# A hybrid decoder step on one core: RMS norms found on the whole row instead of on columns of tokens

## The chip, the core and the metric

The kernel runs on 1 core of a Trainium2 chip. The metric is device time in microseconds (us) for one execution; runs of the kernel before and of a changed kernel are taken on the same chip. The kernel before has a median of 1988.76 us over 3 runs (1988.32 to 1993.46).

## What is computed

One layer of a hybrid decoder for 2048 prompt tokens and 8 sample tokens (2056 in all, 1024 features, float32): RMSNorm; an input projection of 1024 by 1024, whose first half drives a state space mixer (32 groups, 64 complex states) and whose second half a causal pooling mixer; an output projection with residual; RMSNorm; a gated feed-forward part with a causal convolution of width 3 (up to 2 x 2816 columns, down to 1024) with residual; a last RMSNorm. The function at issue is the norm, which stands at three places:

```python
def _rmsnorm(x, g):
    xf = x.astype(jnp.float32)
    y = xf * lax.rsqrt(jnp.mean(xf * xf, axis=-1, keepdims=True) + EPS)
    return (y * g.astype(jnp.float32)).astype(x.dtype)
```

## The kernel before

All activations lie transposed: features on the 128 partitions (8 tiles of them), tokens along the free axis. A token's sum of squares is therefore a sum over 8 tiles and over 128 partitions. Big products are done in three float32r matmuls each (high and low parts, `mm3`, L82 to L89); the parts are made by `split` (L74 to L76: the high part on ScalarE, the low part on VectorE or GpSimd).

The stages, in order of time:

- Start and input projection (to some 300 us). Tokens in 5 pieces (`SUBS`: 512, 512, 512, 264, 256). `prep_x(i)` loads a piece, splits it and finds its norm. For pieces 0 and 1 ScalarE squares each tile and GpSimd adds the squares up per partition (`acc`), and `rstd_from` (L125) turns them into the factor of every token. Pieces 2, 3 and 4 take the sums from rows in natural order (`stats`, L189) and go to `rstd_bcast` (L104) directly. The state space mixer runs in the background of this stage and the next.
- Output projection (some 300 to 605 us). Tokens in 8 pieces (`CSUBS`: 256 each, one of 264). `out_proj(i)` makes x1 tile by tile (L920), squares and sums it (L922 to L926); `norm_out(i)` finds the norm, scales the 8 tiles (L948) and stores them (L950). The last piece's norm is found at once into `rs_last` (L938) and used later.
- Up projection with convolution (some 600 to 1505 us): a Strassen-Winograd scheme with 7 products instead of 8. `prep_h` reloads the normed rows and makes sums and splits of them; `prep_w` does it for the weights.
- Down projection (some 1505 us to the end), 7 products again. `residual` squares and sums the new rows (L1314 to L1321); `final(c)` (L1328) finds the last norm of each of the 8 pieces and scales and stores the output, after the products `p7` (four pieces) and `p4` (four pieces).

`rstd_from` is thus called for 18 norms: 2 of 512 columns, 14 of 256 and 2 of 264. It works on columns of tokens: for each block of 128 tokens, the squares are the weights of a matmul with one column of ones (L133), which puts one token's sum on one partition. `rstd_bcast` then works on 128 x (2 to 4) values: mean and eps (L110), root on ScalarE (L111), reciprocal (L112), one step of Newton (L113 to L116), then per block a diagonal matrix of the factors (L121) and a matmul with ones (L122) that gives every partition all factors, and a copy out of PSUM (L123). The tile of PSUM for both (tag `ms`) exists once, and is shared with the mixer's transposes; the diagonals have two buffers.

The order of each engine's instructions is made by a planner that simulates the program by a cost model and priorities; tiles are reused after their release, and every engine runs its own queue in order. SyncE issues nearly all DMAs, in one queue, in order too.

Of the kernel before, what the change touches and what calls it, by code (L numbers as in the profile page):

```python
# [9 lines left out]
F32 = mybir.dt.float32  # L10
F32R = mybir.dt.float32r
I32 = mybir.dt.int32
AF = mybir.ActivationFunctionType
ALU = mybir.AluOpType
# [4 lines left out]
D = 1024  # L19
# [9 lines left out]
EPS = 1e-6  # L29
# [15 lines left out]
def build(tc, a):  # L45
    nc = tc.nc
    V, S, P, T, Y = nc.vector, nc.scalar, nc.gpsimd, nc.tensor, nc.sync
    es = ExitStack()
    with es:
# [72 lines left out]
                T.matmul(ps[:, b * 128:b * 128 + w], lhsT=ones, rhs=dg[:, :w], start=True, stop=True)  # L122
            S.copy(out=out, in_=ps[:, :n])  # L123

        def rstd_from(accs, out, n):  # L125
            nb = (n + 127) // 128
            ps = psm[0].tile([128, 512], F32, tag="ms", name="ps_st")
            if n % 128:
                V.memset(ps[:, 0:nb], 1.0)
            for b in range(nb):  # L130
                w = min(128, n - b * 128)
                for x, acc in enumerate(accs):
                    T.matmul(ps[0:w, b:b + 1], lhsT=acc[:, b * 128:b * 128 + w], rhs=ones[:, 0:1],  # L133
                             start=x == 0, stop=x == len(accs) - 1)
            rstd_bcast(ps[:, 0:nb], out, n)

        ypair = {}

# [36 lines left out]
        with ExitStack() as er_:  # L175
# [37 lines left out]
            def prep_x(i):  # L213
                t0, n = SUBS[i]
                tiles = []
                nat = i in NAT
                if nat:
                    st = stats(i)
                else:
                    acc = sp.tile([128, 512], F32, tag="dec", name="acc", bufs=2)  # L220
                for k in range(KT):
                    if i < 2:
                        tag = ("H", "tab", "U", "M1", "tm", "yg", "t2", "kt")[k]
                        raw = sp.tile([128, 512], F32, tag=tag, name="xraw", bufs=2 if k < 3 else 1)
                    else:
                        raw = xp.tile([128, 512], F32, tag="xraw", name="xraw", bufs=3)
                    Y.dma_start(out=raw[:, :n], in_=a["xT"][k, :, t0:t0 + n])
                    if i < 4:
                        pool = xp if i % 2 else xpa
                        hi = pool.tile([128, 520], F32R, tag=f"xh{k}", name="xh", bufs=1)  # L230
                        lo = pool.tile([128, 520], F32R, tag=f"xl{k}", name="xl", bufs=1)
                        pair[k] = (hi, lo)
                    else:
                        hi, lo = (t[:, SUBS[3][1]:] for t in pair[k])
                    split_scaled(hi[:, :n], lo[:, :n], raw[:, :n], col(C_G1, k))
                    tiles.append((hi[:, :n], lo[:, :n]))
                    if nat:
                        st(k)
                    elif k == 0:
                        S.activation(out=acc[:, :n], in_=raw[:, :n], func=AF.Square)  # L240
                    else:
                        sq = xp.tile([128, 512], F32, tag="sq", name="sq")
                        S.activation(out=sq[:, :n], in_=raw[:, :n], func=AF.Square)
                        P.tensor_tensor(out=acc[:, :n], in0=acc[:, :n], in1=sq[:, :n], op=ALU.add)
                xr[i] = tiles
                if i == 0:
                    Y.dma_start(out=ident, in_=a["ident"])
                if i < 4:
                    rs = pair["rs"] = xp.tile([128, 520], F32, tag="rstd", name="rstd", bufs=2)
                else:  # L250
                    rs = pair["rs"][:, SUBS[3][1]:]
                if nat:
                    rstd_bcast(st(None), rs[:, :n], n)
                else:
                    rstd_from([acc[:, :n]], rs[:, :n], n)
                rst[i] = rs

            Y.dma_start(out=cst, in_=a["cst"])
# [598 lines left out]
        if True:  # L857
# [14 lines left out]
            def ct(tag, dt=F32, bufs=1, pool=None):  # L872
                return (pool or c2).tile([128, 256 if pool is c3 else CW], dt, tag=tag, name=tag, bufs=bufs)
# [37 lines left out]
            def out_proj(i, g, nxt):  # L911
                t0, n = CSUBS[i]
# [22 lines left out]
                    if i == len(CSUBS) - 1 and d % 2:  # L935
                        Y.dma_start(out=x1_d[i][:, d - 1:d + 1], in_=x1[:, d - 1:d + 1, :n])
                if i == len(CSUBS) - 1:
                    rstd_from([acc[:, :n]], rs_last, n)  # L938
                else:
                    pend.append(lambda: norm_out(i, x1, acc))  # L940

            def norm_out(i, x1, acc):
                t0, n = CSUBS[i]
                Y.dma_start(out=x1_d[i], in_=x1[:, :, :n])
                rs = ct("rs")
                rstd_from([acc[:, :n]], rs[:, :n], n)
                for d in range(KT):
                    V.scalar_tensor_tensor(out=x1[:, d, :n], in0=x1[:, d, :n], scalar=col(C_G2, d), in1=rs[:, :n],  # L948
                                           op0=ALU.mult, op1=ALU.mult)
                Y.dma_start(out=xn_d[i], in_=x1[:, :, :n])  # L950
# [289 lines left out]
        with ExitStack() as ed:  # L1240
# [86 lines left out]
            def final(c, top):  # L1327
# [1 line left out]
                rs = d2.tile([128, 264], F32, tag="rs", name="rs")  # L1329
                low = d2.tile([128, 4, 264], F32, tag="low", name="low")  # L1330
                Y.dma_start(out=low[:, :, :n], in_=x2_d[c])
                rstd_from(ssq[c] if isinstance(ssq[c], list) else [ssq[c][:, :n]], rs[:, :n], n)
                if c == 2 * len(UNITS) - 2:
                    for h, x in enumerate((low, top)):
                        for d in range(4):
# [146 lines left out]
```

## Time and profile before

| | |
|---|---|
| median of 3 runs | 1988.76 us (1988.32 to 1993.46) |
| profiled execution | 1997.34 us, span 1995.5 us |
| TensorE (PE) busy | 1877.3 us, 94% |
| VectorE (DVE) busy | 1404.4 us, 70% |
| ScalarE (ACT) busy | 898.1 us, 45% |
| GpSimd (POOL) busy | 904.7 us, 45% |
| mean granted TensorE clock | 0.973 |

The profile is one execution. The span runs from the first to the last instruction that it records. "Busy" counts an engine's instructions, not waits. An entry in square brackets behind an instruction is the time for which its engine stood idle before it, with what ended that. PEld is TensorE's weight load, SPq a DMA that SyncE issues. Matmuls overlap, so that their spacing, and not their length, says what one costs. A float32 matmul shows as two records.

### The profile page before, as it was taken

The numbers are of one execution on the slowest core, as the hardware profiler recorded it, in microseconds if no ns is written. First come the engines' busy times: TensorE is split into PE (matmuls) and PEld (weight loads), VectorE is DVE, ScalarE is ACT, GpSimd is POOL, SyncE is SP. The second block draws the span as 40 slices with busy tenths as digits, with TensorE's granted clock in tenths as the row PEclk, the third lists the DMA queues.
The fourth block names the chain that finished last, engine by engine and source line by source line (L and its number), as shares of the span: only waits on it lengthen the run. The fifth ranks groups of instructions, "written<-read, shape, count | busy, mean of one in ns | idle before, by whom it ended". The sixth has DMA issues, their size and how long they took to land.

```text
span 1995.5 us, 38363 instructions
## 1 busy us (share of the span) xinstructions
PE 1877.3 (94%) x14680; PEld 1815.0 (91%) x14680; DVE 1404.4 (70%) x2423; ACT 898.1 (45%) x1666; POOL 904.7 (45%) x1091
## 2 busy tenths in 40 slices
PE   6888997999998999999997999999998999999998
PEld 4667876999988999999997999999998989999997
DVE  8888576875588777787789777777775343444675
ACT  5333224544445555555565555555554332322332
POOL 4365662211156455445457555445531165134651
PEclk9989998999999999999998999999998999999999
DMA  6456666865453433233334233323317574356663
GB/s 218 159 165 176 189 179 214 224 176 154 130 178 115 132 122 117 91 112 101 96 102 142 90 114 99 100 87 117 97 60 267 173 248 147 103 189 212 227 205 120
DMA packets 214215, 296.61 MB, mean 149 GB/s; under 512 B 41216, under 2 KB 157824, under 8 KB 213776
## 3 DMA queue, kind: packets, MB, share of 16 engines
q1 hardware_dynamic: 201104, 285.76, 45.3%
q10 hardware_dynamic: 12928, 8.41, 1.5%
q8 instruction: 115, 1.88, 0.4%
q14 instruction: 68, 0.56, 0.1%
HBM read 199.60 MB, written 93.32 MB: 147 GB/s over the span
## 4 chain that ended last, share of the span: by engine, by line
PE 55%; POOL 4%; DVE 4%; DMA 3%; issue 3%; ACT 1%; DVEq 0%; POOLq 0%; ACTq 0%; SPq 0%
PE ps_X L1147 8%; PE ps_X L1146 8%; PE ps_X L1145 8%; PE ps_d L88 4%; PE ps_d L87 4%; PE ps_d L89 4%; PE ps_Z L1146 4%; PE ps_Z L1147 4%; PE ps_Z L1145 4%; PE ps_Y L1147 2%; PE ps_Y L1145 2%; PE ps_Y L1146 2%; DMA x_d<-xo 1%; DMA wr<-w_dn 1%; POOL xo L1307 1%
## 5 line engine op out<-in xcount | busy, mean ns | idle before, releaser
L87 PE MATMUL ps_d<-bh,wh 128*128 128x256 f32 (+1 forms) x1232 | 346.0, 285 | 12.5 <-ACT bh L75 12.5
L88 PE MATMUL ps_d<-bl,wh 128*128 128x256 f32 (+1 forms) x1232 | 349.3, 285 | 6.3 <-DVE bl L76 6.3
L89 PE MATMUL ps_d<-bh,wl 128*128 128x256 f32 (+1 forms) x1232 | 348.5, 284 | 0.0
L76 DVE TENSOR_TENSOR wl<-raw,wh 128x512 fp32r<-128x512 f32 x308 | 270.5, 881 | 64.0 <-ACT wh L75 61.5
L75 ACT CAST wh<-raw 128x512 fp32r<-128x512 f32 x308 | 189.7, 619 | 236.7 <-PE ps_X L1146 166.8
L1173 DVE SCALAR_TENSOR_TENSOR ps_cv<-hup,cst,ps_cv 128x512 f32<-128x512 f32 x352 | 258.1, 750 | 53.1 <-ACT ps_cv L1171 50.9
L1080 POOL TENSOR_TENSOR raw<-raw 128x512 f32<-128x512 f32 x176 | 241.4, 1372 | 83.7 <-DVE wl L76 68.3
L87 PEld LDWEIGHTS ps_d<-bh,wh 128*128 128x128 f32 x1232 | 233.1, 191 | 13.5 <-ACT bh L75 13.5
L88 PEld LDWEIGHTS ps_d<-bl,wh 128*128 128x128 f32 x1232 | 234.7, 191 | 7.4 <-DVE bl L76 7.4
L89 PEld LDWEIGHTS ps_d<-bh,wl 128*128 128x128 f32 x1232 | 235.0, 191 | 0.0
L76 DVE TENSOR_TENSOR bl<-br,bh 128x1536 fp32r<-128x1536 f32 (+3 forms) x56 | 112.4, 2008 | 101.0 <-ACT bh L75 94.0
L1171 ACT ACTIVATE ps_cv<-hup,cst 128x512 f32<-128x512 f32 x176 | 135.9, 782 | 8.3 <-DVE hup L1133 3.9
L87 PE MATMUL ps_in<-xh,wh 128*128 128x512 f32 (+2 forms) x288 | 110.0, 383 | 10.4 <-ACT xh L79 8.1
L926 POOL TENSOR_TENSOR acc<-acc,sq 128x256 f32<-128x256 f32 (+1 forms) x56 | 44.5, 794 | 150.9 <-ACT sq L925 148.6
L88 PE MATMUL ps_in<-xl,wh 128*128 128x512 f32 (+2 forms) x288 | 106.0, 368 | 6.7 <-DVE xl L80 6.7
L1100 POOL TENSOR_TENSOR tt<-cv 128x256 f32<-128x256 f32 (+1 forms) x88 | 79.8, 915 | 61.6 <-DVE cv L1180 28.0
L75 ACT CAST bh<-br 128x1536 fp32r<-128x1536 f32 (+3 forms) x56 | 76.6, 1376 | 66.5 <-PE ps_d L89 65.9
L89 PE MATMUL ps_in<-xh,wl 128*128 128x512 f32 (+2 forms) x288 | 104.3, 363 | 0.1
L1147 PE MATMUL ps_X<-b11h,wl 128*128 128x256 f32 (+1 forms) x352 | 100.0, 284 | 3.1 <-DVE wl L76 3.1
L1146 PE MATMUL ps_X<-b11l,wh 128*128 128x256 f32 (+1 forms) x352 | 99.9, 284 | 2.9 <-DVE b11l L76 2.9
L1145 PE MATMUL ps_X<-bt2h,wh 128*128 128x256 f32 (+1 forms) x352 | 99.9, 284 | 2.5 <-ACT p L1128 2.5
L1146 PE MATMUL ps_Y<-b21l,wh 128*128 128x256 f32 (+1 forms) x352 | 99.3, 282 | 2.5 <-DVE b21l L76 2.5
(436 smaller groups left out, 6476.5 us busy)
## 6 DMA issues: line engine op xcount, KB each, us to landing
raw<-w_up SPq DMA_DIRECT2D x176, 256.0 KB
wr<-w_dn SPq DMA_DIRECT2D x36, 704.0 KB
op_d<-tt SPq DMA_DIRECT2D x33, 512.0 KB
br<-op_d SPq DMA_DIRECT2D x21, 768.0 KB
br<-op_d SPq DMA_DIRECT2D x21, 640.0 KB
op_d<-cv SPq DMA_DIRECT2D x33, 256.0 KB
wr<-w_in SPq DMA_DIRECT2D x16, 512.0 KB
tab<-tab_d SPq DMA_DIRECT2D x32, 256.0 KB
```

The costliest lines, as they stand in the source:

```text
L75: S.copy(out=hi, in_=src)
L76: (eng or V).tensor_tensor(out=lo, in0=src, in1=hi.bitcast(F32), op=ALU.subtract)
L87: T.matmul(ps, lhsT=wh, rhs=rh, start=k == 0, stop=False)
L88: T.matmul(ps, lhsT=wh, rhs=rl, start=False, stop=False)
L89: T.matmul(ps, lhsT=wl, rhs=rh, start=False, stop=k == K - 1)
L1080: P.tensor_tensor(out=r, in0=x, in1=y, op=op)
L1100: P.tensor_tensor(out=o, in0=x, in1=y, op=ALU.subtract)
L1145: T.matmul(ps, lhsT=wh[:, k], rhs=hh[:, k], start=first and k == 0, stop=False, skip_group_check=not first)
L1146: T.matmul(ps, lhsT=wh[:, k], rhs=hl[:, k], start=False, stop=False, skip_group_check=not first)
L1147: T.matmul(ps, lhsT=wl[:, k], rhs=hh[:, k], start=False, stop=k == 3, skip_group_check=not first)
L1171: S.activation(out=c, in_=h[:, o:o + 512], func=AF.Identity, scale=tap(2, jj), bias=col(C_CB, jj))
L1173: V.scalar_tensor_tensor(out=c, in0=h[:, o - 2 + k:o + 510 + k], scalar=tap(k, jj), in1=c, op0=ALU.mult, op1=ALU.add)
```

## The change

`rstd_from` no longer goes through columns of tokens. One product of a 128 x 128 matrix of ones with the sums per partition gives every partition the sums of all tokens of the piece (two such products where there are two sums). Mean, root, reciprocal and the step of Newton are then done at full width, on 128 x 256 (264, 512) values: four operations on VectorE (mean and eps out of PSUM, reciprocal, two products) and three on ScalarE (root, square, and the scale and offset of the step). The result is written straight to its tile; the diagonals, the second product and the copy are gone from these norms. Two scratch tiles of full width are needed: at the start and in the down projection they are taken from the two buffers of the tag of the squares (`sq`), in the output projection from a new tag `rv` with two buffers. `rstd_bcast` stays as it is for the three natural norms.

```diff
-        def rstd_from(accs, out, n):
-            nb = (n + 127) // 128
-            ps = psm[0].tile([128, 512], F32, tag="ms", name="ps_st")
-            if n % 128:
-                V.memset(ps[:, 0:nb], 1.0)
-            for b in range(nb):
-                w = min(128, n - b * 128)
-                for x, acc in enumerate(accs):
-                    T.matmul(ps[0:w, b:b + 1], lhsT=acc[:, b * 128:b * 128 + w], rhs=ones[:, 0:1],
-                             start=x == 0, stop=x == len(accs) - 1)
-            rstd_bcast(ps[:, 0:nb], out, n)
+        def rstd_from(accs, out, n, new):
+
+            ps = psm[0].tile([128, 512], F32, tag="ms", name="ps_st")[:, :n]
+            for x, acc in enumerate(accs):
+                T.matmul(ps, lhsT=ones, rhs=acc, start=x == 0, stop=x == len(accs) - 1)
+            v, s = new()[:, :n], new()[:, :n]
+            V.tensor_scalar(out=v, in0=ps, scalar1=1.0 / D, scalar2=EPS, op0=ALU.mult, op1=ALU.add)
+            S.activation(out=s, in_=v, func=AF.Sqrt)
+            V.reciprocal(out=out, in_=s)
+            S.activation(out=s, in_=out, func=AF.Square)
+            V.tensor_tensor(out=s, in0=s, in1=v, op=ALU.mult)
+            S.activation(out=s, in_=s, func=AF.Copy, scale=-0.5, bias=1.5)
+            V.tensor_tensor(out=out, in0=out, in1=s, op=ALU.mult)
...
-                    rstd_from([acc[:, :n]], rs[:, :n], n)
+                    rstd_from([acc[:, :n]], rs[:, :n], n, lambda: xp.tile([128, 512], F32, tag="sq", name="sq"))
...
-                    rstd_from([acc[:, :n]], rs_last, n)
+                    rstd_from([acc[:, :n]], rs_last, n, lambda: ct("rv", bufs=2))
...
-                rstd_from([acc[:, :n]], rs[:, :n], n)
+                rstd_from([acc[:, :n]], rs[:, :n], n, lambda: ct("rv", bufs=2))
...
-                rstd_from(ssq[c] if isinstance(ssq[c], list) else [ssq[c][:, :n]], rs[:, :n], n)
+                rstd_from(ssq[c] if isinstance(ssq[c], list) else [ssq[c][:, :n]], rs[:, :n], n,
+                          lambda: d2.tile([128, 264], F32, tag="sq", name="sq"))
```

## Rows read from the trace of the kernel before

**Rows 1.** Page: engines' busy time in the span; VectorE in 40 slices.
```profile
PE 1877.3 (94%) x14680; PEld 1815.0 (91%) x14680; DVE 1404.4 (70%) x2423; ACT 898.1 (45%) x1666; POOL 904.7 (45%) x1091
...
DVE  8888576875588777787789777777775343444675
```

**Rows 2.** Windows: stretch, length, busy (instructions) per engine, clock, DMA share, GB/s.
```profile
30.00:65.00 35.00, 27.24 (x113) 20.84 (x112) 32.01 (x157) 14.49 (x36) 4.87 (x8) 0.90 0.45 138
...
450.00:500.00 50.00, 48.01 (x406) 47.84 (x406) 27.17 (x70) 21.80 (x47) 8.10 (x11) 1.00 0.53 151
...
605.00:625.00 20.00, 15.64 (x110) 14.66 (x110) 20.00 (x28) 10.90 (x24) 13.36 (x8) 0.91 0.33 106
...
1870.00:1982.00 112.00, 111.21 (x915) 110.80 (x916) 78.48 (x163) 36.67 (x60) 46.84 (x49) 0.98 0.52 176
```

**Rows 3.** Timeline of TensorE around one norm: start, length, line, operation, count.
```profile
1956.35 0.28 PE L88 MATMUL ps_d<-bl,wh 128*128 128x256 f32 x1
1956.46 0.50 PE L133 MATMUL ps_st<-ones,ss 128*128 128x1 f32 x4
...
1957.03 0.28 PE L87 MATMUL ps_d<-bh,wh 128*128 128x256 f32 x1
...
1961.74 0.61 PE L122 MATMUL ps_rb<-rs_d,ones 128*128 128x128 f32 x4
...
1962.43 0.28 PE L87 MATMUL ps_d<-bh,wh 128*128 128x256 f32 x1
```

**Rows 4.** Timeline of TensorE around a product of the pool map.
```profile
270.41 0.59 PE L697 MATMUL ps_z<-pl,pw__287 128*128 128x256 f32 x2
...
270.96 0.29 PE L88 MATMUL ps_in<-xl,wh 128*128 128x264 f32 x1
```

**Rows 5.** Groups by line and shape, VectorE: count, busy us, mean ns, idle before.
```profile
L1180 DVE TENSOR_TENSOR cv<-cv,ps_cv 128x512 f32<-128x512 f32 x88 | 60.1, 683 | 1.9
...
L121 DVE TENSOR_SCALAR rs_d<-ident,rs_r 128x128 f32<-128x128 f32 x48 | 17.2, 394 | 0.5
...
L114 DVE TENSOR_TENSOR rs_s<-rs_s,rs_v 128x2 f32<-128x2 f32 x15 | 4.5, 300 | 0.4
...
L112 DVE RECIPROCAL rs_r<-rs_s 128x2 f32<-128x2 f32 x15 | 2.5, 164 | 12.1 <-ACT rs_s L111 12.1
...
L110 DVE TENSOR_SCALAR rs_v<-ps_st 128x2 f32<-128x2 f32 x14 | 2.2, 157 | 6.8 <-PE ps_st L133 6.8
...
L468 DVE RECIPROCAL q<-q 128x32 f32<-128x32 f32 x1 | 0.3, 346 | 0.0
```

**Rows 6.** Timelines of VectorE, ScalarE and SyncE: the norm of 264 columns, output projection.
```profile
579.94 0.15 DVE L110 TENSOR_SCALAR rs_v<-ps_st 128x3 f32<-128x3 f32 x1
...
588.85 0.38 ACT L123 COPY rs<-ps_rb 128x264 f32<-128x264 f32 x1 [0.49 <-PE ps_rb L122]
...
595.51 0.32 SPq L950 DMA_DIRECT2D xn_d<-x  x1
...
598.07 0.57 SPq L917 DMA_DIRECT2D xt<-xT  x1
...
602.51 0.42 DVE L920 TENSOR_TENSOR x<-ps_o,xt 128x256 f32<-128x256 f32 x1 [3.96 <-DMA xt<-xT]
```

**Rows 7.** Timeline of ScalarE at the end: the last square and the broadcast's copy.
```profile
1983.70 0.42 ACT L1317 ACTIVATE sq<-V 128x264 f32<-128x264 f32 x1 [0.39 <-POOL ss L1321]
...
1988.49 0.38 ACT L123 COPY rs<-ps_rb 128x264 f32<-128x264 f32 x1 [2.88 <-PE ps_rb L122]
```

**Rows 8.** Timeline of TensorE: instructions with a long wait before them.
```profile
66.10 0.79 PE L87 MATMUL ps_sp<-xh,wh 128*128 128x512 f32 x1 [3.63 <-DVE ut L733]
...
455.93 0.68 PE L122 MATMUL ps_rb<-rs_d,ones 128*128 128x128 f32 x4 [1.99 <-DVE rs_d L121]
...
583.17 1.19 PE L122 MATMUL ps_rb<-rs_d,ones 128*128 128x128 f32 x4 [4.82 <-DVE rs_d L121]
...
624.12 0.68 PE L122 MATMUL ps_rb<-rs_d,ones 128*128 128x128 f32 x4 [1.20 <-DVE rs_d L121]
```

## The prediction

> **What bounds the kernel now.** I began with the page's first two parts: the reader is to see TensorE busy in 94% of the span and VectorE, second, in 70%, but in the first four slices at 8 tenths or more [rows 1]. The share is an average, so I cut the span by stage [rows 2]. Three kinds of place appear. In the output projection and the down projection TensorE does nearly all of every window (48.0 of 50 us, 111.2 of 112 us) and VectorE has room: there a matmul less is time less. At the start (30 to 65 us) and where the up projection begins (605 to 625 us) VectorE is full or nearly so (32.0 of 35, 20.0 of 20) and TensorE waits for it. The end, behind the last matmul of the down projection, is a single chain through one norm. All three hold norms, so each needs its own price. Then I read TensorE's waits in order of time, and SyncE's around 600 us.
>
> **The change part by part.** It touches 18 norms: 2 of 512 columns at the start, 8 in the output projection (one of 264 columns), 8 in the down projection (one of 264). The three norms from natural rows keep the old path.
>
> *TensorE.* A 256-column norm now has two batches of four records. The matmuls around it come 0.12 us apart; the matmul two places behind the first batch starts at 1957.03 instead of 1956.58, the one two places behind the second at 1962.43 instead of 1961.98 [rows 3]: 0.45 us each, 0.90 a norm. The new product is two records, 128x128 by 128x256 in f32. The pool map's product of that shape stands in the trace: it starts at 270.41 and the second matmul behind it at 270.96 instead of 270.53 [rows 4], so 0.43. Saved: about 0.45 us a norm, and one of two places at which the in-order TensorE can be held. Six norms in the output projection (the seventh and eighth fall into the next part) give 2.7 us, seven in the down projection 3.1.
>
> *VectorE.* A 256-column norm now costs 0.157 (mean and eps), 0.164 (reciprocal), four narrow operations of 0.279, 0.300, 0.286 and 0.289, and two diagonals of 0.394: 2.26 us [rows 5] (of the four, the second's row stands there). After: three full-width operations and a full-width reciprocal. A two-operand 128x256 operation out of PSUM takes 0.42 [rows 6], so 1.26 for the three. The reciprocal's width is not in the trace. It was 164 ns at 2 columns and 346 ns at 32, while a product at 2 columns takes about the same as the narrow reciprocal: it pays per column. A line through both points, 6.07 ns a column, gives 1.71 us at 256, 1.75 at 264, 3.26 at 512. The lower end is an operation like any other, 0.42; the upper is 346/32 ns for each column, 2.77 at 256 and 5.5 at 512. I take the line, as it passes through the nearest row. So a norm costs VectorE 2.97 instead of 2.26, 0.7 more (from -0.6 to +1.8). At 512 columns it is three operations of 0.68 [rows 5] and one reciprocal, 5.3, instead of the narrow 1.48 and four diagonals, 3.05: 4.5 more for both norms (-0.7 to +9.0).
>
> The Trainium skill speaks against this edit: "VectorE: DVE Perf Modes", section "Walkthrough: the 8-slice pipeline in each mode", says that the reciprocal is an iterative divide with a repeat count of 8, on a 0.96 GHz engine. Read as 8 cycles a column that is an estimate of 2.13 us at 256 columns, over the line and under the upper end; the two measured widths agree in direction, and by it the sum below would come out some 2.5 us later.
>
> *ScalarE.* A 256-column norm had a root of 0.20 and a copy of 0.37; it gets three full-width operations of 0.42 [rows 7], 0.7 more. ScalarE is at 45% [rows 1], and squares already run between roots without further table loads, so I cost it at nothing where TensorE bounds; the buffered products in PSUM hide it. Were that cover gone, each norm would hold the splits of the next operands for the length of a reciprocal, some 1.7 us.
>
> *The waits.* The new norm goes from VectorE to ScalarE and back three times instead of once. Behind its waiting VectorE instructions are queued the evictions of the projections and the low halves of the splits, for which TensorE waits; that is the cover again. I charge 2 us for it in the output projection and 1.5 in the down projection, one reciprocal each.
>
> *The gates on TensorE.* The broadcast product held TensorE at 455.93 for 1.99 us, at 583.17 for 4.82, at 624.12 for 1.20, each for a diagonal of VectorE [rows 8]. They go. At 455.93 nothing else was late: 2.0 gained. At 583.17 something is late next: the norm's rows are multiplied, stored by SyncE at 595.51, and the last x tile of the projection is queued behind that store (598.07), so that VectorE gets it only at 602.51, after 3.96 us of idleness [rows 6]. What counts is thus when this norm is done. Its mean began at 579.94 and its copy ended at 589.23 [rows 6]; from 579.94 on, seven steps of 0.43, 0.43, 1.75, 0.42, 0.43, 0.42, 0.42 with seven hand-overs of 0.04 make 584.5, some 2.5 us more in a VectorE queue that is full: 587. I take 2.0 of the 4.82 (ends: none, all). At 624.12, with VectorE full and 0.7 to do on top, 0.7 less 0.2 remains: 0.5.
>
> *Start.* VectorE has 3.0 us free in 30 to 65 us [rows 2] and gets 4.5 more: TensorE is held 1.5 longer. Against it the second norm need no longer wait for the first one's broadcast to leave the shared PSUM tile, and TensorE's 3.63 us at 66.10, for the product that this norm scales [rows 8], can shrink. I take +1.5, the hold alone (ends -3.6 and +6.0). The scratch tiles there are those of the squares, two of them: a square of the second norm can wait until the first norm is done. A norm's chain at 512 columns is 3.26, three times 0.68 and three times about 0.7 on ScalarE, 7.4 us, and the second norm's rows are wanted at 66.10 only, so I cost the sharing at nothing; if squares of a later norm take the tiles in between, it is another such chain, which the upper end holds.
>
> *End.* The last square ends at 1984.12, the broadcast's copy at 1988.87 [rows 7]. New: the products 0.05 behind the square and 0.59 long [rows 4], until 1984.78, then 0.42 + 0.42 + 1.75 + 0.42 + 0.42 + 0.42 + 0.42 and seven hand-overs of 0.04 to 0.06: 1989.4, so +0.5 (ends -0.9 and +1.6). By the skill's rule just named it would be +1.0.
>
> *Sum.* -2.7 -3.1 +2.0 +1.5 -2.0 -2.0 -0.5 +1.5 +0.5 = -4.8 us against the profiled execution's 1997.34 us (span 1995.5, 1.84 around it): 1992.5. That execution is 8.6 us over the median of 1988.76; on the median it is **1984**.
>
> **The rivals.** *TensorE gets all of it.* The cover holds everywhere, the second norm at the start comes early enough to cancel VectorE's added work, and the gate at 583 is worth its whole length: -3.1 (seven norms), -3.1, -2.0, -4.8, -1.2, +0.5 = -13.7, so 1975. For it: TensorE's 97% in the projections and the three gates. Against: VectorE is full around the largest gate, so that TensorE's head start meets the same splits.
>
> *VectorE's reciprocals decide.* Place: the windows in which VectorE is full or ends the wait. Price at the upper end: 6.0 at the start, 1.8 at 605 to 625 us, 1.8 for each of three norms of the down projection that fall among large splits (5.4), 1.6 at the end, 14.8 together; TensorE's 14 times 0.45 and the 2.0 of the gate at 455 come off: +6.5, so 1995.3. It decides from about 2.3 us a 256-column reciprocal on. For it: the slope from 2 to 32 columns, and a VectorE that is already busy 70%. Against: in the down projection's last 41 us the norms sit beside a VectorE that is half idle.
>
> *The broadcast was no cost* and nothing else moves: 1989. Against it stand the gates; it lies within my forecast's own range.
>
> **How the numbers follow.** What a measurement of this kernel can tell from no change is about 0.3%, 6 us. My forecast, a small gain that can't be told (1979 to 1993 by itself, the broadcast's rival in it), gets 0.38; TensorE's rival 0.33; VectorE's 0.29. The order of all instructions is planned anew, which can move a stage by some us either way, so the range reaches somewhat beyond both rivals: 1973 to 2000. Faster 0.33, same 0.38, slower 0.29.
>
> **What would show it.** A 256-column reciprocal near 1.7 us (right), near 0.42 or over 2.3 (wrong). No TensorE wait by a diagonal, the second norm's rows well before 66 us, the last x tile's sum before 602 us, TensorE's first 66 us no longer than before. From the end of the last square to the rows: 5.2 us instead of 4.75. If new waits for the low halves of splits appear behind reciprocals, and add up to more than 8 us, the forecast is wrong and VectorE's rival right.

## The result, and the profile after

The changed kernel takes 2006.9 us (median of 4 runs, 2005.5 to 2012.6) against 1988.5 us (4 runs of the kernel before, 1984.3 to 1993.5): a ratio of 1.0089 (95% interval 1.0063 to 1.0115), that is 17.7 us more (12.5 to 22.9); the two medians by themselves differ by 18.4. The forecast was 1984 with a range of 1973 to 2000; it was wrong in sign and the range did not hold the time. The profiled execution took 2012.55 us (span 2010.7). Behind the norm's function its line numbers are higher by 2 than those of before; in the experiments' kernels, which hold both functions, by some more.

The page of the changed kernel first, the engines' busy time and VectorE in 40 slices, as in [rows 1]:

```profile
PE 1861.6 (93%) x14544; PEld 1797.4 (89%) x14544; DVE 1455.4 (72%) x2343; ACT 911.8 (45%) x1685; POOL 907.4 (45%) x1091
...
DVE  8988686786678787878789777777775335344696
```

TensorE's work fell, by 15.7 us, and the span still grew by 15.2: TensorE waits more. VectorE has 80 instructions fewer and is busy 51.0 us longer. The same four windows (TensorE, its weight load, VectorE, ScalarE, GpSimd, then clock, DMA share and GB/s) as in [rows 2]:

```profile
30.00:65.00 35.00, 22.50 (x82) 16.30 (x81) 34.51 (x96) 10.97 (x18) 11.40 (x9) 0.84 0.14 45
450.00:500.00 50.00, 46.73 (x390) 45.71 (x390) 30.91 (x61) 23.91 (x50) 7.67 (x11) 1.00 0.48 140
605.00:625.00 20.00, 9.95 (x65) 9.20 (x65) 14.67 (x27) 6.84 (x17) 9.40 (x12) 0.74 0.43 140
1870.00:1982.00 112.00, 108.01 (x880) 106.77 (x879) 88.50 (x132) 40.35 (x62) 58.33 (x60) 0.98 0.61 204
```

Both places that I had named as VectorE's lost TensorE time, the first 27.24 to 22.50 us and the third 15.64 to 9.95. The windows stand at fixed times, and at 605 us the changed kernel is already some 12 us late, so that the third holds other work than before. The prices of the single operations came out near the forecast. VectorE's groups by line and shape (count, busy us, mean ns), the new reciprocals and the mean at full width; they answer to [rows 5]:

```profile
L133 DVE RECIPROCAL rs<-rv 128x256 f32<-128x256 f32 x6 | 10.5, 1754 | 11.0 <-ACT rv L132 11.0
L133 DVE RECIPROCAL rstd<-sq 128x512 f32<-128x512 f32 x2 | 6.7, 3348 | 0.0
...
L131 DVE TENSOR_SCALAR rv<-ps_st 128x256 f32<-128x256 f32 x7 | 2.9, 420 | 1.4 <-PE ps_st L129 1.4
...
L133 DVE RECIPROCAL rs<-rv 128x264 f32<-128x264 f32 x1 | 1.8, 1803 | 1.9 <-ACT rv L132 1.9
```

TensorE around one norm of 256 columns, as in [rows 3]: the product starts at 1954.05 and the second matmul behind it at 1954.71, 0.66 instead of the usual 0.23, so it costs 0.43 us (the wait of 0.88 ahead of it for the sums not counted) and one batch's 0.45 is saved.

```profile
1954.05 0.70 PE L129 MATMUL ps_st<-ss,ones 128*128 128x256 f32 x2 [0.88 <-POOL ss L1323]
1954.40 0.47 PE L89 MATMUL ps_d<-bh,wl 128*128 128x256 f32 x1
1954.71 0.28 PE L87 MATMUL ps_d<-bh,wh 128*128 128x256 f32 x1
```

What changed is in TensorE's long waits (its timeline, the instructions with a long wait before them), to be read beside [rows 8]. The three waits for a diagonal are gone, and in their place stand longer ones for other things:

```profile
71.12 0.79 PE L87 MATMUL ps_sp<-xh,wh 128*128 128x512 f32 x1 [15.01 <-DVE q L326]
...
317.57 0.58 PE L87 MATMUL ps_g<-yh,wg0h 128*128 128x256 f32 x1 [6.24 <-ACT yh L75]
...
613.69 0.55 PE L1147 MATMUL ps_Y<-b21h,wh 128*128 128x256 f32 x1 [8.67 <-DVE x L922]
...
630.40 0.39 PE L1148 MATMUL ps_X<-b11l,wh 128*128 128x256 f32 x1 [2.52 <-DVE b11l L76]
```

The first is not a wait for `q`: the two evictions of the first half's sums with the second norm's factors (`ut`, L735) come at 69.18 and 70.04, the second ending right before the matmul, because that norm is done at 68.5 us only. VectorE's timeline:

```profile
61.48 3.34 DVE L133 RECIPROCAL rstd<-sq 128x512 f32<-128x512 f32 x1
...
67.86 0.68 DVE L137 TENSOR_TENSOR rstd<-rstd,sq 128x512 f32<-128x512 f32 x1
...
70.04 1.03 DVE L735 TENSOR_TENSOR ut<-ps_sp,rstd 128x512 f32<-128x512 f32 x1
```

At 611, the norm of the 264 columns (VectorE's and SyncE's timelines, as in [rows 6]):

```profile
593.86 0.42 DVE L131 TENSOR_SCALAR rv<-ps_st 128x264 f32<-128x264 f32 x1
596.23 1.80 DVE L133 RECIPROCAL rs<-rv 128x264 f32<-128x264 f32 x1 [1.95 <-ACT rv L132]
...
601.83 0.96 DVE L137 TENSOR_TENSOR rs<-rs,rv 128x264 f32<-128x264 f32 x1
602.83 4.24 DVE L950 SCALAR_TENSOR_TENSOR x<-x,cst,rs 128x264 f32<-128x264 f32 x8
...
613.13 0.41 DVE L922 TENSOR_TENSOR x<-ps_o,xt 128x256 f32<-128x256 f32 x1
614.24 0.42 DVE L922 TENSOR_TENSOR x<-ps_o,xt 128x256 f32<-128x256 f32 x1 [0.70 <-DMA xt<-xT]
```
```profile
607.10 0.32 SPq L952 DMA_DIRECT2D xn_d<-x  x1
607.53 0.36 SPq L919 DMA_DIRECT2D xt<-xT  x1
...
611.20 0.45 SPq L919 DMA_DIRECT2D xt<-xT  x1
```

From its mean to the end of its last step the norm takes 8.9 us here (593.86 to 602.79), against 9.3 before (579.94 to 589.23), and the store and the x tile (`xt`) still queue behind it. TensorE's wait of 8.67 us ends with the eviction at 613.13, the one whose `xt` is loaded right behind the store. The end of the program (ScalarE's and VectorE's timelines, as [rows 7]):

```profile
1998.21 0.42 ACT L1319 ACTIVATE sq<-V 128x264 f32<-128x264 f32 x1 [3.47 <-DVE V L1393]
...
2000.43 1.80 DVE L133 RECIPROCAL rs<-sq 128x264 f32<-128x264 f32 x1 [0.49 <-ACT sq L132]
...
2003.65 0.43 DVE L137 TENSOR_TENSOR rs<-rs,sq 128x264 f32<-128x264 f32 x1 [0.49 <-ACT sq L136]
```

From the end of the last square (1998.63) to the factors (2004.08) 5.45 us, against 4.75 before: +0.7.

### The profile page after: what moved, and what is told of

It reads as the page before. It is cut to its first block, busy times and chain, and to the rows that moved or that the text cites. A ratio compares the mean times of both kernels' runs of the same rounds, so it can differ in the third digit from the quotient of the medians.

```text
span 2010.7 us, 38018 instructions
## 1 busy us (share of the span) xinstructions
PE 1861.6 (93%) x14544; PEld 1797.4 (89%) x14544; DVE 1455.4 (72%) x2343; ACT 911.8 (45%) x1685; POOL 907.4 (45%) x1091
## 5 line engine op out<-in xcount | busy, mean ns | idle before, releaser
L87 PE MATMUL ps_d<-bh,wh 128*128 128x256 f32 (+1 forms) x1232 | 344.8, 284 | 11.8 <-ACT bh L75 11.8
L76 DVE TENSOR_TENSOR wl<-raw,wh 128x512 fp32r<-128x512 f32 x308 | 277.7, 904 | 61.7 <-ACT wh L75 59.2
L1147 PE MATMUL ps_Y<-b21h,wh 128*128 128x256 f32 (+1 forms) x352 | 99.9, 284 | 8.7 <-DVE x L922 8.7
```

The lines of the kernel that those rows point to most:

```text
L76: (eng or V).tensor_tensor(out=lo, in0=src, in1=hi.bitcast(F32), op=ALU.subtract)
L87: T.matmul(ps, lhsT=wh, rhs=rh, start=k == 0, stop=False)
L1147: T.matmul(ps, lhsT=wh[:, k], rhs=hh[:, k], start=first and k == 0, stop=False, skip_group_check=not first)
```

## The experiments

Times are ratios to the kernel before, run on the same chip, turned into us. In brackets stands the 95% interval. To see where a kernel loses, I read the same events in every trace; the table has the delay in us of one profiled execution each against the one of before, whose own times stand in its head: the start of the 8th state of the mixer (`H`), of the first and last eviction of the output projection (`x`), of VectorE's 17th multiply-add of the convolution (`conv 17`), of the down projection's first and last eviction. One execution against another is uncertain by some us: the row "down alone" has the order of before up to 1510 us and is 3.1 us early at 660; the row "one memset more" has it throughout and is 1.7 us late there. The other rows are best read against these two.

```
kernel                    state 8  first x  last x  conv 17  down 1st  down last   timed, us
                          (293.6)  (337.8)  (602.5) (663.4)  (1532.4)  (1983.2)
down alone                  -2.3     -3.3    -3.1     -3.1     -5.0      -6.1      -1.6 [-3.8, 0.6]
changed kernel              +4.9    +11.0   +11.7    +18.0    +19.2     +14.5     +17.7 [12.5, 22.9]
one memset more             -2.0     +0.6    +1.7     +1.7     +2.3      -3.8      +2.2 [-0.6, 4.8]
start alone                 +4.1     +7.6   +10.0    +10.5    +10.3      +3.3     +10.2 [6.8, 13.6]
  without reciprocals       -2.2     +1.3    +3.7     +3.6     +0.5      -5.5      +4.0 [0.8, 7.0]
start in place              +9.7    +16.4   +28.7    +30.4    +28.6     +20.6     +27.5 [23.3, 31.7]
  without reciprocals       +5.2    +10.2   +14.6    +15.0    +15.0      +9.2     +15.3 [12.2, 18.7]
tiles rv alone              -0.4     +6.6    +8.9     +8.9     +6.2      +2.1      +7.6 [4.8, 10.6]
output projection, rv       +0.2     +4.8    +5.0    +12.2    +11.4      +7.7     +10.6 [7.6, 13.8]
output projection, in place -1.9     -2.5    -0.7     +8.4     +4.2      -1.7      +3.2 [0.4, 5.8]
last of its norms alone     -3.4     -3.3    -2.9     +7.4     +2.9      -1.0      +4.0 [1.6, 6.4]
```

### One stage at a time

My theory after the result: the start loses because the first norm takes both tiles of the squares, so that the second piece's squares wait; and the output projection loses by the long chain of the 264-column norm. In the first three runs one stage's norms are new, the other norms go through the old function (kept as `rstd_old`).

```diff
-                    rstd_old([acc[:, :n]], rs[:, :n], n)
+                    rstd_from([acc[:, :n]], rs[:, :n], n, lambda: xp.tile([128, 512], F32, tag="sq", name="sq"))
```

The start alone (the edit above). 

> Only the two 512-column norms at the start are new; the other sixteen are as before. Theory (the scratch tiles are the loss): the first norm takes both tiles of the squares, the second piece's squares wait for it, the last row factor of the second norm is done near 68.5 us instead of 62.3 and TensorE stands some 15 us before 71 us, as in the changed kernel: end of the scaled pool products (last eviction of the projection's first half, 78.6 us before) 5 us later, and the whole +5 to +8 us against before. Rival (a start 5 us late is swallowed later, since VectorE has room behind it): the same 5 us at 80 us, but under +2 us at the end.

Measured: +10.2 us (6.8 to 13.6). The wait before 71 us is there (14.49), the second norm as late as in the changed kernel. It is more than the 5 to 8 us that were expected, though the interval reaches into them, and the rival is out.

```diff
-                rstd_old([acc[:, :n]], rs[:, :n], n)
+                rstd_from([acc[:, :n]], rs[:, :n], n, lambda: ct("rv", bufs=2))
```

The output projection alone (so for `rs_last` too). 

> Only the eight norms of the output projection are new (with their two scratch tiles rv); start and down projection as before. Theory (the long chain of the norm of 264 columns is the loss): the last x tile's sum ends its wait some 10 us later relative to the stage, TensorE stands 7 to 9 us near 605 to 615 us, and the whole is +6 to +8 us. Rival A (the start's delay was only carried there): under +2 us. Rival B (the two scratch tiles move what is laid over their pool's memory and so the stages from 290 us on): the state space stage (290 to 345 us) already +5 us, the whole +10 us or more.

Measured: +10.6 us (7.6 to 13.8). Rival A is out, and rival B's two numbers are what came: the loss is 4.6 us between the 8th state and the first x (294 to 338 us, though no norm is there yet), and there is a second one of 7.2 us between 603 and 663 us.

```diff
-                rstd_old(ssq[c] if isinstance(ssq[c], list) else [ssq[c][:, :n]], rs[:, :n], n)
+                rstd_from(ssq[c] if isinstance(ssq[c], list) else [ssq[c][:, :n]], rs[:, :n], n,
+                          lambda: d2.tile([128, 264], F32, tag="sq", name="sq"))
```

The down projection alone. 

> Only the eight norms of the down projection are new; every instruction ahead of it is in the order of before. Theory (the saved product and diagonals are worth their time there): the down projection takes 464 us as in the changed kernel instead of 470, the whole -4 to -6 us. Rival (the changed kernel's shorter down projection only gave back a delay that its loads had from before): the whole within 2 us of before.

Measured: -1.6 us (-3.8 to 0.6), the rival. What had looked like a shorter down projection in the changed kernel was the profile of before being slow there: from its first eviction to its last it took 450.8 us in the profile of before, 446.1 in the changed kernel, 449.7 here, and 442.8 to 447.1 in the eleven later kernels whose norms there are the old ones. Part of that execution's length is a lower clock. TensorE's timeline of before, and then its window (busy, granted clock):

```profile
1868.90 1.02 PE L133 MATMUL ps_st<-ones,ss 128*128 128x1 f32 x4 [2.56 <-POOL ss L1321]
...
1870.35 0.41 PE L89 MATMUL ps_d<-bh,wl 128*128 128x256 f32 x1
1870.56 0.41 PE L87 MATMUL ps_d<-bh,wh 128*128 128x256 f32 x1
```
```profile
1870.00:1900.00 30.00, 29.92 (x233) 0.91 0.58 197
```

Behind a wait of 2.56 us the matmuls come 0.21 us apart instead of 0.12 [rows 3], the lower of the two clocks. The three stages add up to 19.2, the change to 17.7: each stage can be studied by itself.

### Is it the new order by itself?

An edit can make the planner order everything anew behind it. Two edits with no work worth the name were to tell what that is worth.

```diff
         P.memset(ones, 1.0)
+        P.memset(ones, 1.0)
```

> The kernel before, but GpSimd fills the tile of ones twice (128x128, at the very start, GpSimd has nothing else to do there). The work is the same; the planner's order is not, from the 281st of TensorE's 14342 rows on (some 1100 of VectorE's 2425 rows stand elsewhere). Theory P (a new order of the whole by itself is worth up to 10 us either way): some 4 to 12 us off before, gained or lost in the same places as with the new norms at the start (the two halves of the state space, 300 to 440 us, and the step into the up projection, 600 to 665 us). Rival O (the new norms' own operations are the loss): within 2 us of before.

```diff
+                V.memset(rs[:, 0:1], 0.0)
                 rstd_from([acc[:, :n]], rs[:, :n], n)
```

> The kernel before, with one VectorE memset of one column ahead of each of seven norms of the output projection: under 0.1 us each, 0.7 us in all. The order differs from the 1763rd TensorE row on. Theory P: 4 to 12 us off before, in the places of the run with the output projection's norms alone. Rival O: within 2 us.

Measured: +2.2 us (-0.6 to 4.8) and +0.8 (-1.8 to 3.4). But theory P was not tested by this. The traces show that neither edit made a new order: the added memsets apart, every engine runs the same operations on the same tiles in the same order as before (TensorE's 14680 records, VectorE's 2423, ScalarE's 1666, GpSimd's 1091 and SyncE's 992), but for one copy of GpSimd in the first kernel that stands one place later. The expectations, which say that the order differs, are wrong there. The two runs show how well programs of one order agree, 2 us or so; what a new order by itself is worth stays open. Against it as the cause of the losses below speaks only that they come back in the same places in kernels whose orders differ.

### The two scratch tiles

```diff
                 rs = ct("rs")
+                for _ in range(2):
+                    P.memset(ct("rv", bufs=2)[:, 0:1], 0.0)
                 rstd_from([acc[:, :n]], rs[:, :n], n)
```

The kernel before with the tiles `rv` and no new norm. 

> The kernel before, with the two scratch tiles rv of the changed output projection (2.1 KB a partition) and nothing of its norms: GpSimd writes one column of each, fourteen times under 0.1 us. Theory M (the tiles' memory moves what is laid under them): the state space stage 5 us later, and about +10 us at the end as with the new norms there. Theory P: off by 4 to 12 us either way. Rival O: within 2 us.

```diff
-            v, s = new()[:, :n], new()[:, :n]
-            V.tensor_scalar(out=v, in0=ps, scalar1=1.0 / D, scalar2=EPS, op0=ALU.mult, op1=ALU.add)
+            v, s = ps, accs[0]
+            V.tensor_scalar(out=ps, in0=ps, scalar1=1.0 / D, scalar2=EPS, op0=ALU.mult, op1=ALU.add)
```

The output projection's norms without them. 

> The output projection's eight norms new, but without the scratch tiles rv: the mean stays in the PSUM tile, the root goes into the summed squares' tile. Operations and widths as in the run with the output projection alone. Theory M: 0 to +3 us. Rival O (the longer chain and the reciprocals): +10 us as with rv, TensorE standing 7 us or more at 605 to 615 us. Theory P: off by something between, -5 to +15 us, with the loss in stages that hold no norm too.

Measured: the tiles alone +7.6 us (4.8 to 10.6), the norms without them +3.2 (0.4 to 5.8), with them +10.6. Theory M's numbers came, and the place can be seen. ScalarE's timeline, then SyncE's, of the kernel before with the tiles alone, and TensorE's wait:

```profile
308.83 1.04 ACT L75 CAST wo0h<-wo0r 128x1024 fp32r<-128x1024 f32 x1
309.78 1.04 ACT L75 CAST wo1h<-wo1r 128x1024 fp32r<-128x1024 f32 x1
310.73 0.62 ACT L75 CAST yh<-yr 128x256 fp32r<-128x256 f32 x1
```
```profile
280.71 0.53 SPq L866 DMA_DIRECT2D wo0r<-w_out  x1
...
304.20 0.38 SPq L149 DMA_DIRECT2D yr<-y_d  x1
```
```profile
311.40 0.58 PE L87 MATMUL ps_g<-yh,wg0h 128*128 128x256 f32 x1 [6.25 <-ACT yh L75]
```

And the same queues of the kernel before:

```profile
303.93 0.63 ACT L75 CAST yh<-yr 128x256 fp32r<-128x256 f32 x1 [1.10 <-DMA U<-us_d]
```
```profile
294.92 0.62 SPq L149 DMA_DIRECT2D yr<-y_d  x1
...
311.39 0.58 SPq L866 DMA_DIRECT2D wo0r<-w_out  x1
```

With the tiles, the weights of the output projection are loaded 31 us earlier, ahead of the mixer's output `yr`, which comes 9 us later; ScalarE casts two of them (1.04 each) ahead of `yh`, and TensorE stands 6.25 us for `yh`. The changed kernel has the same wait, 6.24; the run in place has none of it. It is so in every trace: the four kernels that hold the tiles load these weights at 281 to 287 us and wait 5.05 to 6.51 us for `yh`, though three of them have none of GpSimd's memsets; in the others the weights come at 307 us or later, and the longest wait for `yh` in this stretch is 2.12 us. The tiles stand in a pool whose neighbours lie over memory that earlier stages give back; that the weights' tiles come free earlier for this reason is what I take from it, argued and not shown.

### The start

```diff
-                    rstd_old([acc[:, :n]], rs[:, :n], n)
+                    rstd_ip([acc[:, :n]], rs[:, :n], n)
```

`rstd_ip` is the norm in place, as in the diff above. 

> As the run with the start alone, but the two norms take no tile of the squares: the mean stays in the product's PSUM tile and the root goes into the tile of summed squares, which the product has read. Operations, widths and reciprocals are the same. Theory (sharing is the loss): the second piece's squares end near 36 us as before, the second norm's rows come by 60 us, TensorE's wait before 71 us falls from 15 to about 6 us, end of the first half of the projection within 1.5 us of before, the whole 0 to +2 us. Rival (VectorE's two reciprocals of 3.35 us at a full VectorE are the loss): as with the shared tiles, +5 us.

Measured: +27.5 us (23.3 to 31.7). The theory was right for the wait and wrong for the time, which it had at 0 to +2. TensorE's wait (timelines; first the start alone, then the start in place):

```profile
71.72 0.80 PE L87 MATMUL ps_sp<-xh,wh 128*128 128x512 f32 x1 [14.49 <-DVE q L338]
```
```profile
59.52 0.58 PE L87 MATMUL ps_sp<-xh,wh 128*128 128x512 f32 x1 [2.31 <-DVE qr L356]
...
107.47 2.08 PE L724 MATMUL ps_z<-pl,pw__267 128*128 128x512 f32 x2 [5.52 <-DVE pl L704]
```

The projection was 10.6 us ahead at 73 us, and 9.7 us behind when the 8th state began. The windows (stretch, length, busy per engine, clock) of before, and then of this run, show who was full:

```profile
105.00:150.00 45.00, 38.61 (x150) 27.74 (x149) 38.28 (x80) 15.20 (x25) 31.38 (x25) 0.89 0.60 174
```
```profile
105.00:150.00 45.00, 33.89 (x136) 24.44 (x137) 43.38 (x70) 14.70 (x24) 30.19 (x26) 0.82 0.49 138
```

VectorE was busy 43.38 of 45 us: as I read it, TensorE's lead ran into it. So VectorE's own price was tested, with a multiply-add that writes ones in place of the two reciprocals (the norm's value is left out in this and the next run, and in the last one of this part).

```diff
-            V.reciprocal(out=out, in_=s)
+            V.tensor_scalar(out=out, in0=s, scalar1=0.0, scalar2=1.0, op0=ALU.mult, op1=ALU.add)
```

With the tiles of the squares: 

> As the run with the start's two norms alone (shared tiles of the squares), but a multiply-add that writes ones stands where the two 512-column reciprocals were (so the norm's value is left out); only some 25 of VectorE's rows stand elsewhere. Theory S (the shared tiles hold the second piece's squares, whatever the norm costs): a norm's chain is 2.7 us shorter, twice, so TensorE's wait before 71 us falls from 14.5 to about 9, and the whole from +10 to +4 to +6 us. Rival R (VectorE bounds the first 180 us, and all of the loss is the reciprocals' 5.3 us and what follows from them): the first state (177.7 us before, 186.3 with the reciprocals) back at 178, the whole within 3 us of before.

In place: 

> As the run in which the start's two norms work in place (no tile of the squares), again with ones written where the reciprocals were. With them that run was 10 us ahead at 84 us and 27 us behind at the end. Theory R (VectorE bounds the stretch to 180 us, and the reciprocals on it push the state space's tables back): the first state 5 us earlier than 183.5, and the whole +10 us or less instead of +27. Rival L (the early second norm itself turns the planner's order, so that later stages wait for tables and splits, and the reciprocals have no part in it): the first state may move, but the whole stays at +20 us or more.

Measured: +4.0 us (0.8 to 7.0) instead of +10.2, and +15.3 (12.2 to 18.7) instead of +27.5. In the first, nearly nothing else is ordered differently (20 of VectorE's 2411 instructions): two reciprocals of 3.35 us, replaced by operations of 0.43, give back 6.2 us, with some 5 us of uncertainty either way. TensorE's wait falls by as much, from 14.49 to 8.31 us, near the 9 of theory S:

```profile
66.10 0.80 PE L87 MATMUL ps_sp<-xh,wh 128*128 128x512 f32 x1 [8.31 <-DVE q L338]
```

So the reciprocals' length is paid in full, but this run shortens VectorE's load and the chain through the shared tiles together, and doesn't say which of the two is paid. In the second, the first state comes at 173.9 instead of 183.5, as theory R had it, but 15 us remain, so it is only part of that. The traces show one more part. In both runs in place VectorE's busy time in 65 to 150 us is 9 us above that of before (81.7 and 81.8 against 72.6), and 5 and 9 us of that are single instructions that take longer while GpSimd works, as the last section has it. One more run, the first norm old and the second new:

```diff
-                    rstd_from([acc[:, :n]], rs[:, :n], n, lambda: xp.tile([128, 512], F32, tag="sq", name="sq"))
+                    rstd_old([acc[:, :n]], rs[:, :n], n) if i == 0 else rstd_from([acc[:, :n]], rs[:, :n], n, ...)
```

> At the start only the second norm is new, with tiles of the squares as in the changed kernel; the first is old. Theory S (the first norm's use of both tiles holds the second piece's squares): no TensorE wait of 14 us before 71 us, the second norm's rows not later than before, the whole +1 to +5 us, half of the reciprocals' price and none of the sharing's. Rival (the second norm's chain is what counts): the wait stays over 8 us, the whole +7 us or more.

Measured: +7.4 us (4.6 to 10.4). The wait is 4.47 us and the projection 7.2 us ahead at 76 us, as theory S had it; at the first x it is 7.7 us behind like the start alone. That is more than theory S's +1 to +5. So the shared tiles make the 15 us wait, but taking that wait away doesn't bring the time back: of the three kernels without it this one is 2.8 us better, which its interval doesn't tell from nothing, and the two in place are worse. Nor do they lose in one place: the start alone is 8.6 us late at the first state (177.7 us before), this kernel 0.6 there and 6.3 more between the 8th state and the first x. What else than the reciprocals costs 4 us at the start (15 in place) stays open; a new order by itself is not ruled out.

The reciprocals of all 18 norms, in the changed kernel:

> The changed kernel with ones written where all eighteen reciprocals were (the norms' values are left out). Theory (three causes that add up: the shared tiles at the start, the tiles rv, the chain of the 264 columns): rv's 7.5 us and part of the other two stay, the whole +9 to +13 us instead of +18. Rival (the reciprocal's length is the cause of it all): within 3 us of before, or faster.

Measured: +6.8 us (3.8 to 9.8) instead of +17.7, under the +9 to +13 of the theory. The reciprocals are worth 10.9 of the 17.7, with some 6 us of uncertainty. What is left holds the tiles `rv` (the wait for `yh` is there, 5.05 us) and the last norm of the next part, which by themselves cost 7.6 and 4.0: these shares don't simply add.

### The step into the up projection

```diff
-                rstd_ip([acc[:, :n]], rs[:, :n], n)
+                (rstd_old if i == 6 else rstd_ip)([acc[:, :n]], rs[:, :n], n)
```

In place, with the 264-column norm the old way, and the down projection new. 

> Start as before; in the output projection seven norms new and in place (no tiles rv), the norm of the 264 columns the old way; the down projection's eight norms new. Theory N (the long chain of this one norm makes the wait before the up projection): TensorE's wait of 8.1 us at 600.8 us falls to under 5, the up projection begins 1 to 3 us earlier than before, and with the down projection's -1.6 us the whole is -2 to -5 us, ahead of both kernels. Rival V (any new norm in that stretch makes the wait, through VectorE's queue): 6 us or more of wait, the whole +1 to +3 us.

Measured: +5.4 us (2.6 to 8.4), neither: the theory of the 264 columns falls. The wait of 8.1 us before the up projection fell to 4.6, for another thing, but with the old norm its gate came back (4.79 us at 581.5), and the 17th multiply-add of the convolution came 6.9 us late all the same. The last norm (`rs_last`) was left: first it and the 264 columns old, then it alone new.

```diff
-                    rstd_ip([acc[:, :n]], rs_last, n)
+                    rstd_old([acc[:, :n]], rs_last, n)
```

> Six norms of the output projection (256 columns, none of the last two) new and in place, the down projection's eight new, the rest old. Theory E (the last norm's row, given a few us earlier, lets the up projection's first units begin early and out of their order, and the stretch 600 to 665 us then loses 7 us): the wait pattern there is that of before, the 17th convolution input at most 1 us later than in the run with the down projection alone, the whole -1 to -4 us, ahead of both kernels. Rival V (VectorE's longer norms anywhere in the projection): 3 us or more later there, the whole 0 to +5 us.

> Only the last of the output projection's eight norms (256 columns, its rows wanted by the first matmuls of the up projection) new and in place. Theory E: the stretch 600 to 665 us loses 5 to 8 us, the whole +3 to +6 us. Rival V: nothing is lost there, the whole within 2 us of before.

Measured: -0.4 us (-2.8 to 2.0), and +4.0 (1.6 to 6.4) for the last norm alone. The second is theory E's number, and nothing of rival V's; the first lies between the two and tells them apart no further. What does is the stretch from the last x to the 17th multiply-add: 66.6 to 71.2 us in all seven kernels with the last norm new, 60.9 to 62.9 in all eleven with it old, however the rest stands. TensorE's timeline at the up projection's start with the last norm alone new, and then with the last two old:

```profile
617.10 0.39 PE L1173 MATMUL ps_X<-b11l,wh 128*128 128x256 f32 x1 [2.53 <-DVE b11l L76]
619.91 0.58 PE L1173 MATMUL ps_Z<-bt3l,wh 128*128 128x256 f32 x1 [1.26 <-POOL bt3l L76]
```
```profile
616.31 0.39 PE L1173 MATMUL ps_X<-b11l,wh 128*128 128x256 f32 x1 [0.74 <-DVE b11l L76]
...
627.61 0.68 PE L122 MATMUL ps_rb<-rs_d,ones 128*128 128x128 f32 x4 [1.20 <-DVE rs_d L121]
```

With the new norm the first multiply-add of the convolution is 6.5 us earlier than in the run with the down projection alone and the 17th 10.5 later: the planner begins other products there, whose low halves VectorE and GpSimd haven't made. That it does so for want of the gate of 1.20 us is argued and not shown. Part of the 10.5 us is work done earlier (482 of TensorE's matmul records stand in that stretch against 442), so that the timed cost is the smaller 4.0.

### Do the parts add up?

The changed kernel with the output projection in place (`rstd_ip` at its two calls). 

> The changed kernel, all eighteen norms new, but the output projection's work in place, so that the tiles rv are not there. Theory (the parts add up: start +10, output projection in place +3, down projection -1.6): +10 to +13 us instead of +18. Rival (the parts do not add, the planner makes another order of each mixture): 3 us or more outside of that.

Measured: +11.0 us (7.0 to 15.1); the parts +10.2, +3.2 and -1.6 make 11.8. They add up within the intervals. No version beat the kernel before: the down projection's norms alone are the best, -1.6 with an interval that holds nought.

## Why the prediction was wrong, point by point

The sum of the forecast, -4.8 us, stands against +17.7. Its range, widened for a new order, ends 6.9 us under the time.

- **TensorE** (-2.7 and -3.1). 0.45 us a norm was right: the product costs 0.43. In the down projection the whole term with its lost cover and the end, -3.1 + 1.5 + 0.5 = -1.1, stands against a measured -1.6 (-3.8 to 0.6): it fits, but so would no gain at all.
- **Prices on VectorE.** The line through the two narrow reciprocals held: 1.75 us at 256 columns (forecast 1.71), 1.80 at 264 (1.75), 3.35 at 512 (3.26), about 6.2 ns a column from the narrowest to the widest. By the Trainium skill, "VectorE: DVE Perf Modes", section "Walkthrough: the 8-slice pipeline in each mode", a repeat count of 8 read as 8 cycles a column at the 0.96 GHz of its section "Specifications", 256 columns were an estimate of 2.13 us; the trace shows less, 1.75, and it decides.
- **The start, +1.5: the step that failed first.** "TensorE is held 1.5 longer" took 3.0 us of VectorE's free time in 30 to 65 us off the 4.5 that it gets. Measured: +10.2 (6.8 to 13.6), of which the reciprocals' length is about 6: it is paid in full, and the 3.0 us taken off were not there. I read it so that VectorE is loaded not to 65 but to some 150 us (38.28 of 45 us busy in 105 to 150 before, 43.38 in place, once TensorE runs ahead) and that I had cut the window too short. That is not shown: with the start alone VectorE is less busy in 105 to 150 than before (36.55), and what came back with the reciprocals came back as TensorE's wait for the second norm. "I cost the sharing at nothing" was wrong as a mechanism (15 us of wait); as a price it can't be judged, since without the wait the time was no better. The other 4 us stay open.
- **The gates, -2.0, -2.0 and -0.5.** All three waits went, as forecast, and nothing came of it. At 583 I took the norm to be done 2 us earlier; it takes 8.9 us instead of 9.3, because hand-overs that I had at 0.04 us are longer (VectorE stands 1.95 us for ScalarE's root), and the wait (4.82) stands again 18 us later, 8.1 us long in the run in place, for the x tile that queues behind the norm's store. The gate at 624 I took for a cost of 1.20 us, and a gain of 0.5 when it goes: with this one norm new the planner starts the up projection in another order, and it costs 4.0 us.
- **What had no term: memory.** The tiles `rv`, which the change names in one line, cost 7.6 us at 290 to 340 us, where no norm stands. I costed instructions, and no tile. The size is shown, the reason (what is laid over the tiles) is argued.
- **The end, +0.5:** +0.7.

Start +10.2, the tiles +7.6, the last norm +4.0, the other norms of the output and the down projection -0.4 make 21.4; the change measures 17.7 (12.5 to 22.9). The rival "VectorE's reciprocals decide" was nearest, with the sign right, and still 11 us short (+6.5). It had 14.8 us for prices at the upper end, where 10.9 is measured for the reciprocals; but I had it decide from 2.3 us a reciprocal, and they came at 1.75.

## What to carry to other kernels

A new tile is a cost like an instruction: before pricing a change, ask which pools it makes larger and what is laid over them, and try the tiles without the work. Where an engine is nearly full, look how far that stretch reaches, and whether another engine makes its instructions longer there, before its free time is set against the new work. And to tell a new order from a new cost, run an edit that does nothing but change the order, and see in the trace that it did: the two used here left it as it was.

## What was not expected of the hardware

- VectorE's busy time grew by 51.0 us. By the trace's durations the new norms cost 61.7 us and the old ones' instructions some 39, a difference of some 22; the rest lies in instructions that the change doesn't touch (`qr<-qr,q`: 12 of them took 2.2 us before and 6.8 after; the low halves `wl`: 308 took 271.2 and 278.5). The tiles alone, with no work for VectorE, made its busy time 9.0 us longer (1413.4). The traces show with what this goes: GpSimd at work beside it. In the kernel before, 1291 of VectorE's 2423 instructions run beside no instruction of GpSimd, and none of them takes over 0.08 us more than the time within which the fastest fifth of its kind is done (same operation, tiles and shape, in all 18 traces); the others take 183 us more in all, after the change 198. Where the squares of the second piece come late, GpSimd's additions fall among VectorE's small operations: one that takes 0.19 us takes 1.17 beside such an addition and ends with it, at 49.0 us.

```profile
47.64 1.34 POOL L246 TENSOR_TENSOR acc<-acc,sq 128x512 f32<-128x512 f32 x1
```
```profile
47.86 1.17 DVE L326 TENSOR_TENSOR qr<-qr,q 128x32 f32<-128x32 f32 x1
...
50.70 0.19 DVE L326 TENSOR_TENSOR qr<-qr,q 128x32 f32<-128x32 f32 x1
```
- A wait of 2.56 us by TensorE at 1866 to 1869 us was followed by the lower clock (0.91 over the next 30 us); in the run with seven memsets the wait there is 0.91 us and the clock 1.00. One profile can so hold some us that another doesn't.
